# Decoder step on one NeuronCore: two of the four weight sums of a tile pair by accumulating transfers in SBUF, the third as a difference

## The chip, the cores and the metric

The kernel runs on 1 core of one Trainium2 chip. TensorE (PE) multiplies, VectorE (DVE), ScalarE (ACT) and GpSimd (POOL) work on elements, and SyncE (SP) issues most of the DMA transfers. The time is the device time of the program in microseconds. The median of three runs of the kernel before is 1004.09 us (1002.97 to 1006.44).

## The reference

One layer of a hybrid decoder step, all in float32, for a prompt of 512 rows and 8 sequences of 8 rows (576 rows in all), model width 1024:

```python
h = _rmsnorm(x, norm1_g) * (1.0 + sc1) + sh1
proj = h @ w_in
b_gate, c_gate, xa, q, k, v, ga, gb = jnp.split(proj, cuts, axis=-1)
...
yb = o @ w_attn_out
mixed = jax.nn.sigmoid(ga) * ya + jax.nn.sigmoid(gb) * yb
x = x + g1 * (mixed @ w_mix_out)
h2 = _rmsnorm(x, norm2_g) * (1.0 + sc2) + sh2
a, val = jnp.split(h2 @ w_up, 2, axis=-1)
ac, new_ffn = _causal_conv(a, ffn_buf, ffn_conv_w)
x = x + g2 * ((jax.nn.gelu(ac, approximate=False) * val) @ w_down)
```

The change concerns two of these products: the gate logits `ga` and `gb` (16 tiles of 128 columns of `w_in`), and the up projection `h2 @ w_up` (2816 gate columns and 2816 value columns, 22 tiles each).

## The kernel before, in words

Weights come in tiles of 1024 rows by 128 columns, as 128 partitions x 8 blocks x 128 (512 KB); activations stand as 8 slices of 128 partitions x 576. A float32 operand is split into a high part (rounded by ACT) and a low part (the rest, by DVE), and each product takes three passes: high by high, low by high, high by low.

**A pair of tiles.** The gate logits and most of the up projection are computed two column tiles at a time, by a scheme of seven products in place of eight (`pair_product`, L334). For tiles A and B, each cut into its first four blocks (a0, b0) and its last four (a1, b1), and the activations cut likewise and into two halves of 288 columns, it needs the weights a0, a1, b1 and four sums: S1 = b0 + b1, S2 = a0 + S1, S4 = a1 + S2, S3 = a0 + b0. The seven parts use, in this order, a0, S2, S1, a1, b1, S3, S4; each is 4 blocks x 3 passes = 12 matmuls of 288 columns. `pair_product` runs `steps[n]()` behind part n; these steps prepare the weights of the next pair while PE works on this one.

**Preparing a pair** (`pair_weights`, L283). `ra` and `rb` are the two raw tiles. `sums1` makes S3 in a buffer of its own and S1 in place of b0; `sums2` makes S2 in place of a0 and S4 in place of a1; all four are DVE additions of 128x512. Four splits follow, each a high part on ACT (`ah`, `bh`, `ch`, `dh`) and a low part on DVE (`al`, `bl`, `cl`, `dl`): A is (a0, a1), B is (S1, b1), C is (S2, S4), D is S3. A, B and C are 128x1024, D is 128x512. A raw tile may be overwritten by the next load when its last low part is made. The raw buffers are four (`W_BUFS`, L35), so two pairs are held, and the buffers for the tiles of a split are five (`S_BUFS`).

**Where pairs occur.** Eight pairs in the stage of the gates: `gate_raws(n)` loads the two raw tiles, `in_turn` (L329) gives the order of the steps, and a pair's results go through `sigmoid_pair` (DVE combines, ACT sigmoids). Eighteen pairs in the FFN, tiles 4 to 21 of the gate and of the value part (`FfnPair`, L1529). They run in three groups of 4, 8 and 6 pairs (loop at L1707), and behind each group stands a stretch of the down projection. `beside_pair` (L1581) gives the order in which the next pair's preparation and the last pair's elementwise work (first tap, two more taps, GELU, product with the value part, split) stand behind the parts.

**What sets the order.** PE, ACT and DVE are kept in program order in these stages (`pinned`, `InOrder` at L101), so a wait at one instruction holds all that stands behind it on that engine. For SP and POOL a planner sets the order (L1803). All raw tiles are loaded by SP (`load_w`, L145). In these stages POOL does a few 64-column and 16-column operations for each FFN pair and nothing for the gate pairs.

Of the kernel before, what the change touches and what calls it, by code (L numbers as in the profile page):

```python
# [13 lines left out]
ALU = mybir.AluOpType  # L14
AX = mybir.AxisListType

P = 128
D = 1024
NK = D // P
# [50 lines left out]
def step_kernel(ctx: ExitStack, tc: tile.TileContext, ins: dict, outs: list):  # L70
# [43 lines left out]
    pe, act, dve, pool = (InOrder(e) for e in (nc.tensor, nc.scalar, nc.vector, nc.gpsimd))  # L114
# [30 lines left out]
    def load_w(src, nk):  # L145

        raw = wp.tile([P, nk, P], F32, tag="raw", name=nm("raw"), bufs=W_BUFS)
        nc.sync.dma_start(raw, src)
        return raw
# [39 lines left out]
    def drain():  # L189
        while filler:  # L190
            if next(filler[0], True):
                filler.clear()
# [90 lines left out]
    def pair_weights(ra, rb):  # L283

        c0, c1 = slice(0, 4), slice(4, 8)
        w = {}

        def add(out, x, y):
            dve.tensor_tensor(out=out, in0=x, in1=y, op=ALU.add)

        def tiles():
            return [wp.tile([P, NK, P], F32R, tag=t, name=nm(t), bufs=S_BUFS) for t in ("whi", "wlo")]

        def high(name, src, get):
            w[name] = hi, lo = get()
            act.activation(hi, src, AF.Copy)

        def low(name, src):
            hi, lo = w[name]
            dve.tensor_tensor(out=lo, in0=src, in1=hi.bitcast(F32), op=ALU.subtract)  # L300

        def s3_slots():
            return slot("wh", F32R, [P, 4, P]), slot("wl", F32R, [P, 4, P])

        def sums1():
            w["raw"] = slot("s3", shape=[P, 4, P])
            add(w["raw"], ra[:, c0], rb[:, c0])
            add(rb[:, c0], rb[:, c0], rb[:, c1])

        def sums2():  # L310
            add(ra[:, c0], ra[:, c0], rb[:, c0])
            add(ra[:, c1], ra[:, c1], ra[:, c0])

        def named(n0, n1, name):
            hi, lo = w[name]
            w[n0] = (lambda k: hi[:, k, :]), (lambda k: lo[:, k, :])
            if n1:
                w[n1] = (lambda k: hi[:, k + 4, :]), (lambda k: lo[:, k + 4, :])

        def one(name, src, get, n0, n1):  # L320
            return (lambda: (high(name, src(), get), named(n0, n1, name))), (lambda: low(name, src()))

        ah, al = one("A", lambda: ra, tiles, "a0", "a1")
        dh, dl = one("D", lambda: w["raw"], s3_slots, "s3", None)
        bh, bl = one("B", lambda: rb, tiles, "s1", "b1")
        ch, cl = one("C", lambda: ra, tiles, "s2", "s4")
        return w, dict(sums1=sums1, sums2=sums2, ah=ah, al=al, bh=bh, bl=bl, ch=ch, cl=cl, dh=dh, dl=dl)

    def in_turn(t):  # L329

        order = {0: "sums1 ah al", 2: "dh dl sums2", 3: "bh bl", 4: "ch cl"}
        return {at: (lambda names=names: [t[n]() for n in names.split()]) for at, names in order.items()}

    def pair_product(w, x, steps, out_a0, out_a1, out_b0, out_b1):  # L334
# [44 lines left out]
    def kpm(w, m0, k0=0, nk=NK):  # L379
        return w[k0 * P : (k0 + nk) * P, m0 : m0 + P].rearrange("(k p) m -> p k m", p=P)  # L380
# [391 lines left out]
    def queries(t, ps=None):  # L772
# [53 lines left out]
        out=sel,  # L826
# [388 lines left out]
    ya, made = [], {}  # L1215
    wco, wao = ins["w_conv_out"][0], ins["w_attn_out"][0]
    gate_cols = [c + m * P for c in (4608, 5632) for m in range(0, NK, 2)]
    raws = {}

    def gate_raws(n):  # L1220
        if n < len(gate_cols):
            raws[n] = [load_w(kpm(w_in, gate_cols[n] + c), NK) for c in (0, P)]

    def conv_out(m, w):
        ps = product(w, gcv)
        t = slot("ya")
        act.copy(t, ps)
        ya.append(t)
# [6 lines left out]
    w_last = weights(kpm(wco, (NK - 1) * P), NK)  # L1235
    gate_raws(0)
    pinned += [pe, act, dve]
    w, steps = pair_weights(*raws[0])
    steps = in_turn(steps)
    for n in sorted(steps):  # L1240
        steps[n]()
    gate_raws(1)
    conv_out(NK - 1, w_last)
    drain()
    sg, o = [], []
    w_next = {}
# [5 lines left out]
    def gated(m):  # L1252

        if sg[m] is not None:
            dve.tensor_tensor(out=ya[m], in0=ya[m], in1=sg[m], op=ALU.mult)
            sg[m] = None

    for n in range(len(gate_cols)):
        if n + 1 < len(gate_cols):
            gate_raws(n + 2)  # L1260
            after, steps = pair_weights(*raws[n + 1])
            steps = in_turn(steps)
            if n >= 4:
                steps[5] = lambda m=2 * n - 8: gated(m)
                steps[7] = lambda m=2 * n - 7: gated(m)
        else:
            w_next[0] = weights(kpm(wao, 0), NK)
            raw = load_w(kpm(wao, P), NK)
            steps = {
                0: lambda: gated(6), 1: lambda: gated(7), 3: lambda: part_o(2), 4: lambda: part_o(3),  # L1270
                5: lambda: w_next.update({1: split_w(raw)}), 6: lambda: part_o(5), 7: lambda: part_o(7),
            }
        if n + 1 == len(gate_cols):
            fill(modulations(), 2 / 28)
        sg += sigmoid_pair(w, steps)
        w = after
# [17 lines left out]
    def residual(ps, xt, blk, c0=0, c1=NT):  # L1294

        p1 = min(c1, 512)
        dve.scalar_tensor_tensor(
            out=xt[:, c0:p1], in0=ps[:, : p1 - c0], scalar=modT[:, blk, 0:1], in1=xt[:, c0:p1],
            op0=ALU.mult, op1=ALU.add,
        )  # L1300
        if c1 > 512:
            t = sp.tile([P, 64], F32, tag="rt", name=nm("rt"))
            dve.tensor_tensor(
                out=b8(t), in0=b8(ps[:, p1 - c0 :]), in1=bc(modT[:, blk, 1:9]), op=ALU.mult
            )
            dve.tensor_tensor(out=sv(xt), in0=sv(xt), in1=t, op=ALU.add)
# [271 lines left out]
                out[at] = lambda fs=fs: [f() for f in fs]  # L1578
        return out

    def beside_pair(p, t):  # L1581

        none = lambda: None
        f = lambda n: t[n] if t else none
        g = lambda n: getattr(p, n) if p else none
        return {
            0: [f("ah"), g("first_tap"), f("sums1"), f("al"), g("taps")],
            1: [f("dh"), f("bh"), g("gelu")],
            2: [f("dl"), f("sums2"), f("bl"), g("times")],
            4: [f("ch"), g("high"), f("cl"), g("low")],  # L1590
        }

    def down_load(m, m0, m1):
# [46 lines left out]
    def value(t, ps):  # L1640
        t.times(ps)
        t.high()
# [35 lines left out]
    low()  # L1678
    ops[2].low()
    steps = pair.prepare()  # L1680
    nxt = FfnPair(5)
    ops[3].sums()
    ops[3].high()
    steps["ah"]()
    a3 = product(w_a3, h2)
    value(tiles[2], v2)
    tiles[2].low()
    ops[3].low()
    steps["sums1"]()
    steps["al"]()  # L1690
    steps["dh"]()
    steps["bh"]()
    steps["dl"]()
    v3 = product(w_v3, h2)
    start(tiles[3], a3)
    steps["sums2"]()
    tiles[3].taps()
    tiles[3].gelu()
    steps["ch"]()
    steps["bl"]()  # L1700
    steps["cl"]()
    value(tiles[3], v3)
    tiles[3].low()
# [3 lines left out]
    for m0, m1 in FCH:  # L1707
# [3 lines left out]
        for m in range(max(m0, 4), m1):  # L1711
            pair = pairs.pop(m)
            beside = [{0: n3}] if m == 4 else []
            if m + 1 < m1:
                if m + 2 < m1:
                    pairs[m + 2] = FfnPair(m + 2)
                beside.append(beside_pair(before, pairs[m + 1].prepare()))
            else:
                wd = {}
                raw = [down_load(j, m0, m1) for j in range(2)]  # L1720
                beside.append(beside_pair(before, None))
                beside.append({2: [lambda: wd.update({0: split_w(raw[0])})],
                               4: [lambda: wd.update({1: split_w(raw[1])})]})
            pair.run(merged(*beside))
            before = pair
# [6 lines left out]
        if m1 < NF:  # L1732
            pairs = {m1: FfnPair(m1)}
            steps = None
            ps = [mmps() for _ in range(2)]
            n = m1 - m0
            for k0, k1 in ((0, n - 2), (n - 2, n)):
                for j in range(2):
                    for k in range(k0, k1):
                        kstep(halves(ps[j]), wd[j], fa, k)  # L1740
            wd[2] = split_w(down_load(2, m0, m1))
            for j in range(2):
                residual(pf(ps[j]), x1[j], 40 + j)
            for m in range(2, NK):
                if m + 1 < NK:
                    wd[m + 1] = split_w(down_load(m + 1, m0, m1))
                acc_m = product(wd[m], fa)
                if m == 4:
                    steps = in_turn(pairs[m1].prepare())
                    steps[0]()  # L1750
                elif m > 4:
                    steps[m - 3]()
                if m == NK - 1:
                    pairs[m1 + 1] = FfnPair(m1 + 1)
                residual(acc_m, x1[m], 40 + m)
            continue
        pinned.clear()
# [77 lines left out]
```

## Time and profile before

| What | us |
|---|---|
| Median of three runs | 1004.09 |
| The profiled execution, its own time | 1004.44 |
| Its span, first to last instruction | 1002.6 |
| PE busy in the span | 982.7 |
| DVE busy | 670.3 |
| ACT busy | 442.3 |
| POOL busy | 85.7 |
| Gate pairs: 386.7 to 475.7 | 89.0 |
| FFN pairs 4 to 7: 645.1 to 690.3 | 45.2 |
| FFN pairs 8 to 15: 741.0 to 831.1 | 90.1 |
| FFN pairs 16 to 21: 881.9 to 945.7 | 63.8 |

The stretches at the bottom are read from the starts of the matmuls in the timeline. A view of groups has the line, the engine, the operation, the output and the inputs by the program's names, the shape and the count; "idle before" is time in which the engine had nothing to do ahead of the instruction, with what ended it. Nearly all DVE, ACT and PE work is shown at L109, the line of the helper that keeps engines in order, so groups are told apart by tiles: `raw` is a raw weight tile or a sum made in its place, `s` the buffer of S3, `whi` and `wlo` the split parts of A, B and C, `wh` and `wl` those of S3, `uv`, `p`, `pad`, `sg` and `cy` the combinations of the seven products. SPq and POOLq are DMA issues.

### The profile page before, as it was taken

Reading aid. Unit: us, or ns where it says so; the run is one execution under the profiler, and the core shown is the slowest. Engines: PE = TensorE matmul, PEld = TensorE weight load, DVE = VectorE, ACT = ScalarE, POOL = GpSimd, SP = SyncE. Lnnn points to the kernel's source line nnn. Section 1 sums busy time; section 2 is a strip of 40 time slices with the busy share of each in tenths; the row PEclk is TensorE's granted clock in tenths of the full one; section 3 lists DMA queues with packets and bytes.
Section 4 is the critical chain, followed back from the end, with each engine's and each line's share of the span. In section 5 each row is a group of like instructions: output and inputs, shape, how many; then the busy total and the mean of one; then the engine's idle time right before and its main releaser. Section 6 shows DMA issues by size and latency. Waiting matters only on the chain.

```text
span 1002.6 us, 18686 instructions
## 1 busy us (share of the span) xinstructions
PE 982.7 (98%) x7502; PEld 941.9 (94%) x7502; DVE 670.3 (67%) x1244; ACT 442.3 (44%) x831; POOL 85.7 (9%) x241
## 2 busy tenths in 40 slices
PE   7999999999999999999999999999999999999996
PEld 5898999999989889999889999999999999999996
DVE  5736766665653367888463568896559995579944
ACT  5454545444534335454242348554225543235433
POOL 2210000000010000000000022011001110001121
PEclk9999999999999999999999999999999999999999
DMA  9993323333413932225973302223233322323302
GB/s 285 321 251 99 96 75 86 86 115 106 152 58 83 304 106 84 85 86 154 359 213 87 109 1 74 75 84 107 78 97 96 88 85 85 105 64 100 117 24 95
DMA packets 176424, 119.70 MB, mean 119 GB/s; under 512 B 8943, under 2 KB 162766, under 8 KB 176050
## 3 DMA queue, kind: packets, MB, share of 16 engines
q1 hardware_dynamic: 174482, 111.06, 37.4%
q0 software_dynamic: 1856, 7.44, 2.1%
q8 instruction: 59, 0.97, 0.4%
q14 instruction: 27, 0.22, 0.1%
HBM read 109.69 MB, written 7.35 MB: 117 GB/s over the span
## 4 chain that ended last, share of the span: by engine, by line
PE 86%; DVE 7%; ACT 2%; DMA 2%; issue 1%; SPq 0%; POOL 0%; DVEq 0%; ACTq 0%
PE mm L109 62%; PE aux L109 21%; DVE wlo L109 2%; PE aux L1099 2%; PE aux L1014 1%; DMA raw<-in_w_in 1%; DVE raw L109 1%; DMA ad<-in_w_ada 1%; DMA q<-low 1%; DVE cy L109 0%; ACT whi L109 0%; DVE y L109 0%; DVE uv L109 0%; SPq L385 0%; DMA con<-in_consts 0%
## 5 line engine op out<-in xcount | busy, mean ns | idle before, releaser
L109 ACT ACTIVATE whi<-raw 128x1024 fp32r<-128x1024 f32 (+2 forms) x164 | 168.0, 1034 | 200.7 <-PE mm L109 109.4
L109 DVE TENSOR_TENSOR wlo<-raw,whi 128x1024 fp32r<-128x1024 f32 (+2 forms) x164 | 195.2, 1195 | 46.9 <-ACT whi L109 45.2
L109 PE MATMUL mm<-hh,whi 128*128 128x256 f32 (+2 forms) x560 | 127.7, 305 | 0.6 <-ACT hh L109 0.6
L109 PE MATMUL mm<-hh,wlo 128*128 128x256 f32 (+2 forms) x560 | 122.3, 295 | 0.0
L109 PE MATMUL mm<-hl,whi 128*128 128x256 f32 (+2 forms) x560 | 121.1, 295 | 0.0
L109 PEld LDWEIGHTS mm<-hh,whi 128*128 128x128 f32 x560 | 91.7, 189 | 8.3 <-issue 6.6
L109 PEld LDWEIGHTS mm<-hh,wlo 128*128 128x128 f32 x560 | 94.3, 188 | 0.0
L109 PEld LDWEIGHTS mm<-hl,whi 128*128 128x128 f32 x560 | 93.7, 188 | 0.4 <-DVE hl L109 0.4
L109 DVE SCALAR_TENSOR_TENSOR x<-mm,modT,x 128x512 f32<-128x512 f32 (+1 forms) x33 | 22.6, 685 | 79.0 <-PE mm L109 79.0
L109 PE MATMUL mm<-fl,whi 128*128 128x256 f32 (+1 forms) x304 | 65.3, 296 | 0.0
L109 PE MATMUL mm<-fh,wlo 128*128 128x256 f32 (+1 forms) x304 | 65.1, 295 | 0.0
L109 PE MATMUL mm<-fh,whi 128*128 128x256 f32 (+1 forms) x304 | 65.1, 296 | 0.0
L109 PE MATMUL mm<-th,whi 128*128 128x288 f32 x208 | 61.8, 297 | 0.6 <-DVE uv L109 0.5
L109 PE MATMUL mm<-th,wlo 128*128 128x288 f32 x208 | 61.5, 296 | 0.5 <-DVE wlo L109 0.5
L109 PE MATMUL mm<-tl,whi 128*128 128x288 f32 x208 | 61.4, 295 | 0.0
L109 PEld LDWEIGHTS mm<-fl,whi 128*128 128x128 f32 x304 | 51.0, 189 | 0.0
L109 PEld LDWEIGHTS mm<-fh,wlo 128*128 128x128 f32 x304 | 50.9, 188 | 0.1
L109 PEld LDWEIGHTS mm<-fh,whi 128*128 128x128 f32 x304 | 50.6, 188 | 0.1
L109 PE MATMUL aux<-2h,whi 128*128 128x288 f32 (+2 forms) x160 | 47.4, 296 | 0.8 <-ACT p L109 0.8
L109 PE MATMUL aux<-2h,wlo 128*128 128x288 f32 (+2 forms) x160 | 47.5, 297 | 0.0
L109 PE MATMUL aux<-2l,whi 128*128 128x288 f32 (+2 forms) x160 | 47.2, 295 | 0.0
L865 ACT ACTIVATE s<-s,nmx 128x256 f32<-128x256 f32 (+1 forms) x72 | 34.0, 475 | 27.4 <-DVE nmx L862 27.4
(302 smaller groups left out, 2547.5 us busy)
## 6 DMA issues: line engine op xcount, KB each, us to landing
raw<-in_w_in SPq DMA_DIRECT2D x52, 512.0 KB, 4.8
raw<-in_w_up SPq DMA_DIRECT2D x44, 512.0 KB, 3.9
ada<-in_w_ada SPq DMA_DIRECT2D x64, 256.0 KB, 6.0
ad<-in_w_ada SPq DMA_DIRECT2D x32, 256.0 KB, 6.5
raw<-in_w_down SPq DMA_DIRECT2D x16, 512.0 KB, 3.6
raw<-in_w_conv_out SPq DMA_DIRECT2D x8, 512.0 KB, 3.6
raw<-in_w_attn_out SPq DMA_DIRECT2D x8, 512.0 KB, 3.6
raw<-in_w_mix_out SPq DMA_DIRECT2D x8, 512.0 KB, 5.8
```

The lines of the kernel that those rows point to most:

```text
L109: done = getattr(self.engine, name)(*args, **kwargs)
L865: nc.scalar.activation(s[x // 2][:, x % 2, :w], s[x // 2][:, x % 2, :w], AF.Exp, bias=nmx[:, x : x + 1], accum_out=den[:, x : x + 1],)
L1014: done = nc.tensor.matmul(O[HALF[par], :256], vt(i - nkt + 1 + kt)[:, hd * 64 : hd * 64 + 64], pts[kt][:, par * 256 : par * 256 + 256], st ...
L1099: done = nc.tensor.matmul(ps[32 * j : 32 * j + 32, :], cT[:, k, :], cols[k][j], start=(k == 1), stop=(k == NK - 2),)
```

## The change

S1 and S4 are no longer DVE additions. Each becomes a transfer from SBUF to SBUF that adds into its destination, issued by POOL: S1 adds b1 into b0, and S4 adds S2 into a1. S2 stays a DVE addition, and now needs S1. S3 is now a DVE subtraction, S2 - b1, which equals a0 + b0. The order of the steps follows: for the gates A and S2 come first, then S3 and B, then D, then C (before: S3, S1 and A, then D, S2 and S4, then B, then C). S1 of a pair is issued one pair earlier, behind part 6 of the gates and behind part 5 of the FFN pairs. So the next pair's loads and `pair_weights` are called earlier in the program. In the gates the multiplications `gated` move from part 5 to part 3 for the first of two.

```diff
-        def add(out, x, y):
-            dve.tensor_tensor(out=out, in0=x, in1=y, op=ALU.add)
+        def add_to(out, x):
+            pool.dma_start(out, x, accum_op=ALU.add)
...
-        def sums1():
+        def s1():
+            add_to(rb[:, c0], rb[:, c1])
+
+        def s2():
+            dve.tensor_tensor(out=ra[:, c0], in0=ra[:, c0], in1=rb[:, c0], op=ALU.add)
+            add_to(ra[:, c1], ra[:, c0])
+
+        def s3():
             w["raw"] = slot("s3", shape=[P, 4, P])
-            add(w["raw"], ra[:, c0], rb[:, c0])
-            add(rb[:, c0], rb[:, c0], rb[:, c1])
-
-        def sums2():
-            add(ra[:, c0], ra[:, c0], rb[:, c0])
-            add(ra[:, c1], ra[:, c1], ra[:, c0])
+            dve.tensor_tensor(out=w["raw"], in0=ra[:, c0], in1=rb[:, c1], op=ALU.subtract)
...
-        order = {0: "sums1 ah al", 2: "dh dl sums2", 3: "bh bl", 4: "ch cl"}
+        order = {0: "ah al s2", 2: "s3 bh bl", 4: "dh dl", 5: "ch cl"}
...
+            first_sum = prep[n + 2][1]["s1"] if n + 2 in prep else lambda: None
             if n >= 4:
-                steps[5] = lambda m=2 * n - 8: gated(m)
+                steps[3] = lambda m=2 * n - 8: gated(m)
                 steps[7] = lambda m=2 * n - 7: gated(m)
+            steps[6] = first_sum
...
-            0: [f("ah"), g("first_tap"), f("sums1"), f("al"), g("taps")],
-            1: [f("dh"), f("bh"), g("gelu")],
-            2: [f("dl"), f("sums2"), f("bl"), g("times")],
-            4: [f("ch"), g("high"), f("cl"), g("low")],
+            0: [f("ah"), g("first_tap"), f("al"), f("s2"), g("taps")],
+            1: [f("bh"), g("gelu")],
+            2: [f("s3"), f("bl"), g("times")],
+            4: [f("dh"), g("high"), f("dl"), g("low")],
+            5: [f("ch"), f("cl"), after["s1"] if after else none],
...
                 elif m > 4:
-                    steps[m - 3]()
+                    steps[2 * m - 10]()
                 if m == NK - 1:
+                    steps[5]()
                     pairs[m1 + 1] = FfnPair(m1 + 1)
+                    pairs[m1 + 1].prepare()["s1"]()
```

The rest of the diff places the same steps around the first pair of each stage.

More of the change, by code (lines that the diff above doesn't have):

```diff
@@ L326, in pair_weights @@
         ch, cl = one("C", lambda: ra, tiles, "s2", "s4")
-        return w, dict(sums1=sums1, sums2=sums2, ah=ah, al=al, bh=bh, bl=bl, ch=ch, cl=cl, dh=dh, dl=dl)
+        return w, dict(s1=s1, s2=s2, s3=s3, ah=ah, al=al, bh=bh, bl=bl, ch=ch, cl=cl, dh=dh, dl=dl)
     def in_turn(t):
-        order = {0: "sums1 ah al", 2: "dh dl sums2", 3: "bh bl", 4: "ch cl"}
+        order = {0: "ah al s2", 2: "s3 bh bl", 4: "dh dl", 5: "ch cl"}
         return {at: (lambda names=names: [t[n]() for n in names.split()]) for at, names in order.items()}
@@ L1217, in step_kernel @@
     gate_cols = [c + m * P for c in (4608, 5632) for m in range(0, NK, 2)]
-    raws = {}
+    prep = {}
     def gate_raws(n):
         if n < len(gate_cols):
-            raws[n] = [load_w(kpm(w_in, gate_cols[n] + c), NK) for c in (0, P)]
+            prep[n] = pair_weights(*[load_w(kpm(w_in, gate_cols[n] + c), NK) for c in (0, P)])
     def conv_out(m, w):
@@ L1237, in step_kernel @@
     pinned += [pe, act, dve]
-    w, steps = pair_weights(*raws[0])
+    w, steps = prep[0]
+    steps["s1"]()
     steps = in_turn(steps)
@@ L1243, in step_kernel @@
     conv_out(NK - 1, w_last)
+    prep[1][1]["s1"]()
     drain()
@@ L1260, in step_kernel @@
             gate_raws(n + 2)
-            after, steps = pair_weights(*raws[n + 1])
+            after, steps = prep[n + 1]
             steps = in_turn(steps)
+            first_sum = prep[n + 2][1]["s1"] if n + 2 in prep else lambda: None
             if n >= 4:
-                steps[5] = lambda m=2 * n - 8: gated(m)
+                steps[3] = lambda m=2 * n - 8: gated(m)
                 steps[7] = lambda m=2 * n - 7: gated(m)
+            steps[6] = first_sum
         else:
@@ L1579, in merged, with beside_pair @@
         return out
-    def beside_pair(p, t):
+    def beside_pair(p, t, after=None):
         none = lambda: None
@@ L1680, in step_kernel @@
     steps = pair.prepare()
+    steps["s1"]()
     nxt = FfnPair(5)
@@ L1686, in step_kernel @@
     value(tiles[2], v2)
+    steps["al"]()
+    steps["s2"]()
     tiles[2].low()
     ops[3].low()
-    steps["sums1"]()
-    steps["al"]()
-    steps["dh"]()
     steps["bh"]()
-    steps["dl"]()
+    steps["bl"]()
+    steps["s3"]()
     v3 = product(w_v3, h2)
     start(tiles[3], a3)
-    steps["sums2"]()
+    steps["dh"]()
+    steps["ch"]()
+    steps["dl"]()
     tiles[3].taps()
     tiles[3].gelu()
-    steps["ch"]()
-    steps["bl"]()
+    nxt.prepare()["s1"]()
     steps["cl"]()
@@ L1714, in step_kernel @@
             if m + 1 < m1:
+                after = None
                 if m + 2 < m1:
                     pairs[m + 2] = FfnPair(m + 2)
-                beside.append(beside_pair(before, pairs[m + 1].prepare()))
+                    after = pairs[m + 2].prepare()
+                beside.append(beside_pair(before, pairs[m + 1].steps, after))
             else:
@@ L1749, in step_kernel @@
                     steps = in_turn(pairs[m1].prepare())
-                    steps[0]()
+                    pairs[m1].steps["s1"]()
                 elif m > 4:
-                    steps[m - 3]()
+                    steps[2 * m - 10]()
                 if m == NK - 1:
+                    steps[5]()
                     pairs[m1 + 1] = FfnPair(m1 + 1)
+                    pairs[m1 + 1].prepare()["s1"]()
                 residual(acc_m, x1[m], 40 + m)
```

## The prediction

> **What bounds the kernel now.** I read the page first (its span and busy lines), then the busy time of each engine by stretch, then the timeline of PE inside the FFN stretches.
>
> ```profile
> span 1002.6 us, 18686 instructions
> PE 982.7 (98%) x7502; PEld 941.9 (94%) x7502; DVE 670.3 (67%) x1244; ACT 442.3 (44%) x831; POOL 85.7 (9%) x241
> ```
> ```profile
> 386.70:475.70 89.00, 89.00 (x674) 89.00 (x673) 74.33 (x109) 45.95 (x74) 0.00 (x0) 1.00 0.38 114
> 641.00:690.30 49.30, 47.82 (x357) 47.15 (x357) 45.83 (x72) 25.27 (x39) 6.64 (x22) 1.00 0.34 97
> 741.00:831.10 90.10, 89.60 (x674) 89.16 (x673) 85.69 (x135) 46.28 (x67) 12.37 (x43) 1.00 0.30 89
> 881.90:945.70 63.80, 63.80 (x484) 63.76 (x482) 60.27 (x96) 33.26 (x49) 8.17 (x28) 1.00 0.26 75
> ```
>
> The columns of the second fence are the stretch and its length, then busy time and count of PE, PEld, DVE, ACT and POOL, the granted clock, the DMA share and GB/s. The clock is 1.00 everywhere, so it plays no part. PE is the bound: the eight gate pairs take 89.00, 11.13 us for a pair of 84 matmuls. In the gates PE never idles, so DVE work taken out there can gain nothing. In the FFN stretches DVE is nearly full, and PE has small holes. These are the holes (start, length, operation; in brackets the idle time and what ended it):
>
> ```profile
> 645.20 0.29 PE L109 MATMUL mm<-tl,whi 128*128 128x288 f32 x1
> 646.03 0.40 PE L109 MATMUL mm<-th,wlo 128*128 128x288 f32 x1 [0.54 <-DVE wlo L109]
> ...
> 650.04 0.40 PE L109 MATMUL aux<-2h,whi 128*128 128x288 f32 x1 [0.82 <-ACT p L109]
> ...
> 680.22 0.29 PE L109 MATMUL aux<-2h,wlo 128*128 128x288 f32 x1
> 680.63 0.37 PE L109 MATMUL mm<-th,whi 128*128 128x288 f32 x1
> ...
> 809.37 0.29 PE L109 MATMUL aux<-2h,wlo 128*128 128x288 f32 x1
> 809.90 0.37 PE L109 MATMUL mm<-th,whi 128*128 128x288 f32 x1 [0.23 <-DVE uv L109]
> ...
> 820.96 0.29 PE L109 MATMUL aux<-2h,wlo 128*128 128x288 f32 x1
> 821.52 0.37 PE L109 MATMUL mm<-th,whi 128*128 128x288 f32 x1 [0.26 <-DVE uv L109]
> ```
>
> Matmuls follow each other every 0.13 us (89.00 / 674), so the starts lost are 0.83 - 0.13 = 0.70, about 0.9 (0.82 idle and a slower first matmul), 0.28, 0.40 and 0.43, in all 2.7; with a slower first matmul behind the first ones as well some 3.2. **That is the ceiling of any gain**: 0.32% of the time.
>
> **Part 1: the additions leave DVE.** One FFN pair on DVE, from product to product (start, length, operation):
>
> ```profile
> 787.22 0.45 DVE L109 TENSOR_TENSOR uv<-mm,uv 128x288 f32<-128x288 f32 x1
> 787.59 0.68 DVE L109 TENSOR_TENSOR s<-raw,raw 128x512 f32<-128x512 f32 x1
> 788.31 0.69 DVE L109 TENSOR_TENSOR raw<-raw 128x512 f32<-128x512 f32 x1
> 788.92 1.22 DVE L109 TENSOR_TENSOR wlo<-raw,whi 128x1024 fp32r<-128x1024 f32 x1
> ...
> 792.63 0.80 DVE L109 TENSOR_TENSOR raw<-raw,raw 128x512 f32<-128x512 f32 x1
> 793.47 0.69 DVE L109 TENSOR_TENSOR raw<-raw 128x512 f32<-128x512 f32 x1
> 794.08 1.22 DVE L109 TENSOR_TENSOR wlo<-raw,whi 128x1024 fp32r<-128x1024 f32 x1
> ...
> 798.84 0.45 DVE L109 TENSOR_TENSOR uv<-mm,uv 128x288 f32<-128x288 f32 x1
> ```
>
> DVE's period is 798.84 - 787.22 = 11.62 against PE's 11.13, so DVE falls back by 0.5 us a pair until PE waits for `uv`. The four sums take 788.92 - 787.59 = 1.33 and 794.08 - 792.63 = 1.45. Two stay (2 x 0.69), so the period becomes 11.62 - 2.78 + 1.38 = 10.22, below PE's. The stalls at 680, 809 and 821 end in `uv` and are a result of that drift; they go: 0.28 + 0.40 + 0.43 = 1.1, with the refill some 1.35. Of the two at the entry to the first FFN group, which wait for `wlo` and ACT's `p`, I take 1.0 of about 1.85, since the entry has the same steps with two sums fewer. Gain: 2.4.
>
> **Part 2: 52 transfers come onto POOL's queue.** Two for each of 26 pairs. POOL's own cost for one is its issue, of which there is a row:
>
> ```profile
> 478.02 0.55 POOL L1325 DMA_DIRECT2D x<-xT_dram  x1 [147.19 <-DVE ol L109]
> ```
>
> 52 x 0.55 = 28.6 us on an engine that is busy 85.7 of 1002.6; it waits anyway, so nothing for throughput. But order on POOL counts: for each pair it first issues S1 of the pair after next, which waits for that raw tile's load, and then S4 of the next pair. A late load therefore holds S4, and behind S4 stand the 64-column operations (`cy`) of the FFN.
>
> **Part 3: how long one lasts, L.** No accumulating transfer and none from SBUF to SBUF is in the trace. Its time from issue to landing is bounded by these rows (output and input, queue, count, KB each, median us to landing):
>
> ```profile
> raw<-in_w_up SPq DMA_DIRECT2D x44, 512.0 KB, 3.9
> xT_dram<-xT POOLq DMA_DIRECT2D x4, 576.0 KB, 6.1
> x<-xT_dram POOLq DMA_DIRECT2D x2, 1152.0 KB, 8.5
> out<-yo SPq DMA_DIRECT2D x8, 256.0 KB, 2.3
> out<-so POOLq DMA_DIRECT2D x7, 32.0 KB, 1.8
> ```
>
> The transfer has 256 KB, 128 x 512 float32. From below 2.3, the same bytes out of SBUF on SP's queue with no reading of the destination. From above 6.1, a POOL transfer of 576 KB, a little more than the 512 KB that are read (source and destination). In between, the POOL rows of 32 KB (1.8) and 1152 KB (8.5) give 6.7 / 1120 = 0.0060 us per KB; with 512 KB read, 1.8 + 512 x 0.0060 = 4.9. I take 4.9, because it is the one that uses POOL's queue at this size and counts both operands; with 256 KB alone the same line gives 3.3. DMA itself is not full (0.26 to 0.38).
>
> The Trainium skill ("DMA: Bandwidth & Descriptors", Anatomy of one DMA — SWDGE (gpsimd) path) fits a GpSimd transfer as 2.0 us plus its bytes at 436 GB/s; as an estimate 2.6 us here, between the rows' ends, and by it the time would be that of rival 1 below. The fit is for transfers that do not add, and no run before shows one that does.
>
> **Part 4: the new wait in the gates.** Before, C was made from S2 and S4 of DVE, one behind the other. Now `s4` is on the way for L, and ACT's `ch` waits for it, DVE's `cl` for `ch`. DVE and ACT are in program order. Behind `cl` stand the combinations of the pair that PE has just finished (v, b0, b1, then a1), behind these the sigmoid on ACT and the next `ah`, `al`, `s2`, and then the next `s4`: a loop over one pair. Its links (the last two rows are groups: count, busy and mean ns, then idle before):
>
> ```profile
> 440.99 0.45 DVE L109 TENSOR_TENSOR uv<-mm,p 128x288 f32<-128x288 f32 x1
> ...
> 441.84 0.45 DVE L109 TENSOR_TENSOR sg<-uv,p 128x288 f32<-128x288 f32 x1
> ...
> 442.56 0.46 DVE L109 TENSOR_TENSOR sg<-mm,uv 128x288 f32<-128x288 f32 x1 [0.27 <-PE mm L109]
> ```
> ```profile
> 442.38 1.12 ACT L109 ACTIVATE sg<-sg 128x576 f32<-128x576 f32 x2 [3.23 <-issue]
> 443.40 1.05 ACT L109 ACTIVATE whi<-raw 128x1024 fp32r<-128x1024 f32 x1
> ```
> ```profile
> L109 DVE TENSOR_TENSOR raw<-raw 128x512 f32<-128x512 f32 x14 | 9.7, 692 | 0.5
> L109 DVE TENSOR_TENSOR wlo<-raw,whi 128x1024 fp32r<-128x1024 f32 x24 | 29.4, 1224 | 8.8 <-ACT whi L109 8.4
> ```
>
> ch 1.05, cl 1.22, v to b1 1.30 (440.99 to 442.29), a1 0.46, then from 443.02 (a1's end) to 444.45 (`ah`'s end) 1.43, al 1.22, s2 0.69: 7.37, and about 0.3 of hand-offs between engines: 7.7 + L. Against 11.13 it is hidden up to **L = 3.4**. At 4.9 the loop takes 12.6, and each turn loses 1.47.
>
> How much of that is free the first time: PE starts a run of pairs at 386.70 + 5 x 11.125 = 442.33, and `ah` ends 443.40 + 1.05 - 442.33 = 2.1 into the run, so `s4` goes out at 2.1 + 1.22 + 0.69 = 4.05, and `cl` ends at 4.05 + 4.9 + 1.05 + 1.22 = 11.2. PE needs the bank that v clears at the second part of the next pair, 11.13 + 12 x 0.13 = 12.7, v takes 0.45: limit 12.2. Slack 0.95 us. Pairs 1 to 7 are made inside the loop, so six turns follow the first: 6 x 1.47 - 0.95 = **7.9 us lost**. With the slack the loss over all turns is 7 L - 26.4, so it begins at L = 3.8, not at 3.4.
>
> **Part 5: the loads' loop in the FFN.** The elementwise work of an FFN pair stands ahead of `ch`, so the loop above does not close there (DVE's 10.22 leaves room). Another does: a raw tile is free when `cl` has read it, then 3.9 for the load of the tile that takes its place, POOL's issue of S1 that waits for it 0.55, then `s4` behind it on the same queue L, ch 1.05, cl 1.22: 6.7 + L, hidden up to 4.4. At 4.9 it is 11.6, 0.5 too long; four turns in the group of eight lose 2.0, two in the group of six 1.0. The first `cl` ends at about 5.2 + 4.9 = 10.1, 2.1 ahead of the same limit: **nothing lost**, the load's lead is used up. Before, that lead was large:
>
> ```profile
> 785.50 0.37 SPq L148 DMA_DIRECT2D raw<-in_w_up  x1
> ```
>
> 785.50 + 4.9 (this one's own landing, later than the median) is 790.4, and the next pair needs it near 797.
>
> **The sum.** Part 1 -2.4, part 2 0, part 4 +7.9, part 5 0: +5.5. On the profiled execution, 1004.44 by its own time (span 1002.6), 1009.9; it stands 0.35 above the median, so **1009.6** against 1004.09.
>
> **Rivals.** 0.3% is 3.0 us, about what a measurement of this kernel tells from no change; faster means below 1001.1, slower above 1007.1.
>
> *Rival 1, the other side: the transfers are hidden.* If L is at most 3.8, both loops fit, the gates' with their slack, and only part 1 is left: 1004.1 - 2.4 = 1001.7, or 1000.9 when all 3.2 of the holes close. For it: 256 KB from SP land in 2.3, and one operand only on POOL's line gives 3.3. Against it: POOL's 576 KB took 6.1, and the add reads twice the bytes. It decides at L = 3.8. Chance 0.30, of which 0.12 falls below 1001.1 and 0.18 within 0.3%.
>
> *Rival 2: the FFN's loads chain too.* From L = 5.5 on. At 5.5 the gates lose 7 x 5.5 - 26.4 = 12.1, the FFN group of eight 4 x 1.07 - 1.5 = 2.8 and the group of six 2 x 1.07 - 1.5 = 0.6: 15.5 - 2.4 = +13.1, 1017. At the upper end 6.1: 16.3, 4 x 1.67 - 0.9 = 5.8 and 2.4, less 2.4: +22.1, 1026. For it: S1 and S4 go out close together on one queue while two loads of 512 KB run, and 6.1 was measured when four POOL transfers ran close together. Chance 0.22.
>
> *Rival 3: POOL's issue itself is slowed by DVE*, which is busy 84 to 95% in these stretches; the 0.55 row fell in a stretch where it was not. If an issue waits for one or two splits (1.22 each), L becomes 6.1 to 7.3; each 1 us costs 7 in the gates and 4 + 2 in the FFN: 1026 to 1042. Nothing in the trace speaks for it. Chance 0.06.
>
> That the DVE additions would not go away is excluded: the program of the changed kernel has 52 of them fewer. That they go and gain nothing, as PE's holes stay at the entries, is inside the first rival (1004).
>
> **How the numbers follow.** Forecast 0.42 (L from 3.8 to 5.4, where the same sums give 1002 to 1015; 0.06 of it within 0.3%), rival 1 0.30, rival 2 0.22, rival 3 0.06. Faster 0.12; same 0.18 + 0.06 = 0.24; slower 0.64. The range runs from rival 1 with nearly all holes closed, 1001.0, to rival 2 at its upper end, 1027. The likeliest case alone spans 1002 to 1015.
>
> **What would show it.** In the DMA issues, `raw` from `raw` on POOL's queue, 26 twice, with L. DVE busy near 670.3 - 26 x 1.4 = 634. In the gates PE's time for a pair above 11.13 from the third or fourth on, holes at the second part that end in DVE's `uv`, ACT's `whi` waiting for the DMA. In the FFN, no holes at 680, 809, 821. Wrong if L is below 3.8 (gates stay 89.0), if `s1` waits for its load ahead of `s4` so long that POOL's order and not L sets the loop, or if the clock in these stretches falls below 1.00.

## The result, and the profile after

The changed kernel takes 1014.84 us (median of 4 runs, 1013.34 to 1017.39) against 1003.53 of the kernel before. The ratio on record, 1.0104 with a 95% interval of 1.008 to 1.0127, lies a little below the quotient of these two medians, 1.0113. A second set of six runs (below, `e9_changed_again`) gave 1012.04 against 1004.13, ratio 1.0082 (1.0061 to 1.0104). So it is slower by about 8 to 11 us; 1009.6 was predicted. The profiled execution took 1013.83, span 1011.7: 9.1 above the span before.

The page of the changed kernel: span, busy times, and the group and the DMA row of the new transfers (count, busy and mean ns, idle before; then KB each and median us to landing):

```profile
span 1011.7 us, 18812 instructions
...
PE 985.4 (97%) x7502; PEld 943.9 (93%) x7502; DVE 637.6 (63%) x1192; ACT 442.0 (44%) x831; POOL 140.0 (14%) x293
...
L109 POOL DMA_DIRECT2D raw<-raw x52 | 45.2, 903 | 277.5 <-DVE raw L109 78.4
...
raw<-raw POOLq DMA_DIRECT2D x52, 256.0 KB, 3.4
```

Busy times by stretch (columns as in the prediction):

```profile
386.70:475.70 89.00, 85.74 (x638) 84.77 (x638) 56.42 (x84) 42.51 (x67) 11.02 (x13) 1.00 0.56 127
641.00:690.30 49.30, 46.51 (x349) 46.08 (x348) 39.93 (x62) 25.48 (x40) 14.33 (x30) 1.00 0.51 116
741.00:831.10 90.10, 88.48 (x665) 87.87 (x664) 73.11 (x113) 42.72 (x61) 27.90 (x55) 1.00 0.57 133
881.90:945.70 63.80, 63.80 (x483) 63.66 (x482) 50.55 (x79) 30.45 (x44) 19.21 (x38) 1.00 0.56 130
```

DVE is 33 us less busy, as the change means. The holes that it was to close in the FFN are closed, but PE has new ones, and for the first time some in the gates (timeline of PE):

```profile
435.96 0.37 PE L109 MATMUL mm<-th,whi 128*128 128x288 f32 x1 [0.77 <-DVE uv L109]
448.10 0.37 PE L109 MATMUL mm<-th,whi 128*128 128x288 f32 x1 [0.69 <-DVE uv L109]
460.37 0.37 PE L109 MATMUL mm<-th,whi 128*128 128x288 f32 x1 [0.88 <-DVE uv L109]
...
664.30 0.37 PE L109 MATMUL mm<-th,whi 128*128 128x288 f32 x1 [0.90 <-DVE uv L109]
...
677.54 0.37 PE L109 MATMUL mm<-th,whi 128*128 128x288 f32 x1 [1.89 <-DVE uv L109]
...
807.59 0.37 PE L109 MATMUL mm<-th,whi 128*128 128x288 f32 x1 [0.74 <-DVE uv L109]
```

All end in DVE's `uv`: the second part of a pair waits for the combination v of the last one, as the prediction had it. Setting each matmul's start against the same matmul before tells where the 9.1 us are. Some 1.8 stand ahead of the change, 1.5 of them at 86 to 90 us, where the granted clock was 0.57 in this execution (not in the second one). The gates and their exit lose 5.2 (4.8 up to 475.7). The entry to the FFN gains 1.9. The first FFN group then loses 2.9 net, the group of eight 1.2 net of the holes of before that are gone, the group of six nothing.

**The chain in the gates.** One turn on POOL, ACT and DVE of the changed kernel:

```profile
452.19 0.84 POOL L109 DMA_DIRECT2D raw<-raw  x1 [10.15 <-DVE wlo L109]
453.38 0.85 POOL L109 DMA_DIRECT2D raw<-raw  x1 [0.35 <-DVE uv L109]
```
```profile
457.54 1.06 ACT L109 ACTIVATE whi<-raw 128x1024 fp32r<-128x1024 f32 x1 [3.05 <-DMA raw<-raw]
...
469.80 1.06 ACT L109 ACTIVATE whi<-raw 128x1024 fp32r<-128x1024 f32 x1 [3.10 <-DMA raw<-raw]
```
```profile
452.16 0.69 DVE L109 TENSOR_TENSOR raw<-raw,raw 128x512 f32<-128x512 f32 x1
...
458.63 1.23 DVE L109 TENSOR_TENSOR wlo<-raw,whi 128x1024 fp32r<-128x1024 f32 x1 [2.41 <-ACT whi L109]
459.77 0.45 DVE L109 TENSOR_TENSOR uv<-mm,p 128x288 f32<-128x288 f32 x1
```

S2 ends at 452.85, `s4` goes out at 453.38 (0.53 later) and `ch`, waiting for it, starts at 457.54 (4.16 later); then `cl`, then v at 459.77, and PE goes on at 460.37. One turn is 469.80 - 457.54 = 12.26 us against PE's 11.13; the prediction had 12.6. The first POOL row is S1 of the pair after next, ahead of S4 on the queue.

**The chain in the FFN.** SP's load, POOL's two issues (x2 is S1 and S4), then ACT and SP's next load:

```profile
795.03 0.37 SPq L148 DMA_DIRECT2D raw<-in_w_up  x1
...
807.11 0.37 SPq L148 DMA_DIRECT2D raw<-in_w_up  x1
```
```profile
799.46 1.78 POOL L109 DMA_DIRECT2D raw<-raw  x2 [3.05 <-DMA raw<-in_w_up]
```
```profile
804.76 1.06 ACT L109 ACTIVATE whi<-raw 128x1024 fp32r<-128x1024 f32 x1 [1.09 <-DMA raw<-raw]
```

POOL waited for the load, not for S2, which had ended at 798.39. S1 went out at 799.46, S4 at 800.04, and `ch` started 4.72 later. From load to load it is 12.08 us: the loop of the prediction's part 5, at 11.6 there.

The first FFN group, where the largest hole is (677.54), shows the same pair of issues (x2) and the wait behind them:

```profile
668.38 1.78 POOL L109 DMA_DIRECT2D raw<-raw  x2 [3.19 <-DMA raw<-in_w_up]
```
```profile
674.71 2.00 ACT L109 ACTIVATE whi<-raw 128x1024 fp32r<-128x1024 f32 x2 [2.18 <-DMA raw<-raw]
```

S1 went out at 668.38, S4 at 669.10, and `ch` could start at 674.71 only.

### The profile page after: what moved, and what is told of

The parts are those of the page before. It is cut to its first block, busy times and chain, and to the rows that moved or that the text cites. A ratio compares the mean times of both kernels' runs of the same rounds, so it can differ in the third digit from the quotient of the medians.

```text
span 1011.7 us, 18812 instructions
## 1 busy us (share of the span) xinstructions
PE 985.4 (97%) x7502; PEld 943.9 (93%) x7502; DVE 637.6 (63%) x1192; ACT 442.0 (44%) x831; POOL 140.0 (14%) x293
## 4 chain that ended last, share of the span: by engine, by line
PE 69%; DMA 10%; DVE 7%; ACT 4%; issue 4%; POOL 1%; DVEq 0%; POOLq 0%; ACTq 0%
PE mm L109 54%; PE aux L109 13%; DMA raw<-raw 5%; DVE wlo L109 3%; ACT whi L109 2%; PE aux L1102 2%; DMA raw<-in_w_up 2%; DMA raw<-in_w_in 1%; PE aux L1017 1%; DMA snk<-in_attn_sinks 1%; DVE uv L109 1%; DMA q<-low 1%; ACT sg L109 0%; DVE ol L109 0%; DVE y L109 0%
## 5 line engine op out<-in xcount | busy, mean ns | idle before, releaser
L109 POOL DMA_DIRECT2D raw<-raw x52 | 45.2, 903 | 277.5 <-DVE raw L109 78.4
L109 PEld LDWEIGHTS mm<-th,whi 128*128 128x128 f32 x208 | 39.1, 188 | 9.8 <-ACT whi L109 5.1
```

The lines of the kernel that those rows point to most:

```text
L109: done = getattr(self.engine, name)(*args, **kwargs)
```

## The experiments

The theory from these two chains was that the loss is what waits for S4's transfer, and S1 ahead of it on POOL's queue makes that wait longer (the flight theory). Against it stood the new order of the steps (order theory) and the bytes moved inside SBUF (traffic theory).

**S1 by transfer, S4 on DVE.**

```diff
-            add_to(ra[:, c1], ra[:, c0])
+            dve.tensor_tensor(out=ra[:, c1], in0=ra[:, c1], in1=ra[:, c0], op=ALU.add)
```

> S4 goes back to DVE, S1 stays a transfer; the order of the steps is that of the changed kernel. Flight theory (the loss comes from what waits for S4's transfer: its flight of about 4.0 us, and in the FFN S1 ahead of it on POOL's queue): nothing waits for S1, which is issued one pair early, and DVE has one addition less (11.62 - 0.69 = 10.9 us a pair, below PE's 11.13). Both the gates' 5 us and the FFN's 3.5 us of loss go, the gain of the FFN's holes stays: 2 to 3 us below the kernel before, 1001 to 1002. Order theory (the new order of the steps, S3 as a difference and C last, makes the loss): as slow as the changed kernel, 1011 to 1015. Traffic theory (the bytes moved inside SBUF slow loads and engines): half of the bytes, half of the loss, 1007 to 1010.

Measured 1003.22 against 1004.24, ratio 0.9983 (0.9971 to 0.9995); span 1001.4. The gates have no hole (PE 89.00 of 89.00), the loss is gone, with half of the transfers. But only 1.2 us is gained in the stages of the change by the starts of the matmuls, where 2 to 3 were expected. DVE's period, from `uv` to `uv`, is still 11.61, as before, though it has one addition less:

```profile
809.75 0.45 DVE L109 TENSOR_TENSOR uv<-mm,uv 128x288 f32<-128x288 f32 x1
...
821.36 0.45 DVE L109 TENSOR_TENSOR uv<-mm,uv 128x288 f32<-128x288 f32 x1
```

**S4 by transfer, S1 on DVE** (where DVE waits for ACT anyway).

```diff
-            add_to(rb[:, c0], rb[:, c1])
+            dve.tensor_tensor(out=rb[:, c0], in0=rb[:, c0], in1=rb[:, c1], op=ALU.add)
...
+        al = lambda: (s1(), al_())
```

> S1 goes back to DVE, ahead of the low part of A, where DVE waits for ACT; S4 stays a transfer. Flight theory: with no S1 ahead of it on the queue, S4 lands 3.3 us after its issue in place of 4.0 to 4.6, the gates' loop falls from 12.2 to 11.5 us, which its slack covers but for 0 to 1 us, and in the FFN no transfer waits for a load: 1001 to 1003. Order theory: 1011 to 1015. Traffic theory: half of the loss, 1007 to 1010. If S4's flight is 4.0 whether or not S1 is ahead of it, the gates keep their 4.5 us and the time is 1005 to 1007.

Measured 1005.92, ratio 1.0019 (1.0005 to 1.0033): better than the changed kernel by 6 to 9 us, but above what was expected. A turn in the gates is now the distance of two POOL rows:

```profile
437.30 0.84 POOL L109 DMA_DIRECT2D raw<-raw  x1 [10.82 <-DVE uv L109]
448.98 0.85 POOL L109 DMA_DIRECT2D raw<-raw  x1 [10.84 <-DVE uv L109]
```

It is 11.68, and the flight is 3.5 (448.98 to 452.53). That is still longer than PE's 11.13, so the last three pairs lose 0.3 to 0.6 us each; the rest is lost at the exit of the gates and in the first FFN group, where a hole of 1.2 us stands at the second pair.

**All sums on DVE, in the new order.**

```diff
         def s1():
-            add_to(rb[:, c0], rb[:, c1])
+            pass
         def s2():
+            dve.tensor_tensor(out=rb[:, c0], in0=rb[:, c0], in1=rb[:, c1], op=ALU.add)
             dve.tensor_tensor(out=ra[:, c0], in0=ra[:, c0], in1=rb[:, c0], op=ALU.add)
-            add_to(ra[:, c1], ra[:, c0])
+            dve.tensor_tensor(out=ra[:, c1], in0=ra[:, c1], in1=ra[:, c0], op=ALU.add)
```

> All sums on DVE, in the order of the changed kernel (S3 as a difference, C last, S1 and S4 on either side of S2 on DVE). Flight theory and traffic theory: no transfer, no loss, and DVE as full as before (11.62 us a pair), so the holes of the kernel before are there again: 1002 to 1006. Order theory: 1011 to 1015.

Measured 1011.53, ratio 1.0074 (1.0061 to 1.0087). This speaks for the order theory, but elsewhere than the changed kernel loses:

```profile
386.70:475.70 89.00, 89.00 (x674) 89.00 (x673) 72.54 (x106) 45.92 (x73) 0.00 (x0) 1.00 0.35 104
...
741.00:831.10 90.10, 86.86 (x648) 85.82 (x647) 82.19 (x128) 43.84 (x63) 14.82 (x40) 1.00 0.30 88
```
```profile
790.70 0.45 DVE L109 TENSOR_TENSOR uv<-mm,uv 128x288 f32<-128x288 f32 x1
...
800.61 1.23 DVE L109 TENSOR_TENSOR wlo<-raw,whi 128x1024 fp32r<-128x1024 f32 x1 [0.19 <-ACT whi L109]
...
802.91 0.45 DVE L109 TENSOR_TENSOR uv<-mm,uv 128x288 f32<-128x288 f32 x1
```

The gates have no hole at all, so their loss in the changed kernel isn't the order's. In the FFN DVE's period is 802.91 - 790.70 = 12.21 with the same four sums that took 11.62 before: the new order costs DVE 0.6 us a pair, partly in waits for ACT's high parts (0.19 here, 0.21 at `fl`). It fits only when DVE has less to do, which also explains the first experiment: 12.21 - 0.6 or so for one addition is 11.6. The expectation had put this at nothing.

**S4 ahead of S1 on POOL's queue.** All 52 transfers stay; POOL keeps the program's order, in which S4 of the next pair comes first. This holds for POOL's small operations in the FFN too.

```diff
-    pinned += [pe, act, dve]
+    pinned += [pe, act, dve, pool]
...
-            pinned.extend([dve, act])
+            pinned.extend([dve, act, pool])
```

> The changed kernel with POOL's transfers kept in the order of the program: S4 of the next pair goes out before S1 of the pair after it, which no longer stands ahead of it on the queue. All 52 transfers stay. Flight theory: S4's flight falls from 4.0 to 4.6 to about 3.3, the gates' loop to 11.5, and in the FFN S4 no longer waits for a load; 1001 to 1003.5. Order theory and traffic theory: no change against the changed kernel, 1011 to 1015. If only the FFN recovers, as S4's flight does not depend on S1, 1007 to 1010.

Measured 1003.96, ratio 1.0008 (0.9992 to 1.0023); span 1000.2, 2.4 below the kernel before, of which 1.9 stand ahead of the change. This settles most of it: the same transfers and the same order on PE, ACT and DVE, and the loss is gone but for the end of the gates.

```profile
386.70:475.70 89.00, 88.06 (x661) 87.66 (x660) 63.09 (x94) 44.34 (x71) 11.15 (x13) 1.00 0.62 137
...
741.00:831.10 90.10, 90.10 (x683) 90.10 (x683) 79.71 (x122) 47.12 (x67) 22.97 (x58) 1.00 0.59 132
```
```profile
447.43 1.72 POOL L109 DMA_DIRECT2D raw<-raw  x2 [9.87 <-DVE uv L109]
...
459.35 0.84 POOL L109 DMA_DIRECT2D raw<-raw  x1 [10.20 <-ACT sg L109]
```

The group of eight is full (90.10 of 90.10), more than before (89.60). In the gates S4 now flies 3.4 us (447.43 to 450.83), a turn is 11.6 to 11.9, and PE loses 1.3 us at the last two pairs, when the slack is used up. The traffic theory falls: the transfers are all there. Their traffic isn't free, though: the S1 that follows S4 lands 5.3 us after its issue, and a load of 512 KB that starts 1.1 us behind it in the gates takes 5.75 us, where most such loads took 4.1 to 4.3 in the changed kernel; neither is waited for.

**S4 first, and in the gates on DVE.**

```diff
+            if gates:
+                dve.tensor_tensor(out=ra[:, c1], in0=ra[:, c1], in1=ra[:, c0], op=ALU.add)
+            else:
                 add_to(ra[:, c1], ra[:, c0])
```

> The changed kernel with S4 ahead of S1 on POOL's queue as in e4_s4_first, and in the gates S4 on DVE as in e1_s1_only; in the FFN both sums stay transfers. If the gates' loss is the flight of S4 alone, the gates show no hole (1.4 us less than e4_s4_first), and the FFN has e4_s4_first's gain of 2 to 3 us: 1001 to 1002, 2 to 3 us below the kernel before. If the S1 transfers hurt the gates by their traffic, 1 us of holes stays in the gates and the time is 1002.5 to 1004.

Measured 1002.75 against 1003.85, ratio 0.9985 (0.9971 to 1.0); span 999.7. The gates have no hole:

```profile
386.70:475.70 89.00, 89.00 (x671) 89.00 (x670) 70.12 (x101) 45.83 (x74) 5.05 (x6) 1.00 0.44 119
641.00:690.30 49.30, 48.73 (x368) 48.48 (x367) 42.33 (x67) 25.22 (x39) 10.81 (x27) 1.00 0.59 140
741.00:831.10 90.10, 90.10 (x682) 90.10 (x682) 79.65 (x121) 47.13 (x67) 22.73 (x58) 1.00 0.59 132
```

The span is 2.9 us shorter, 0.45 of it ahead of the change and some 0.2 behind the last matmul. By the starts of the matmuls the stages of the change gain 2.2, near the 2.4 that the prediction had put for part 1: 2.7 in the FFN, less 0.45 in the gates, which are slower by 0.06 us a pair without a hole. The runs with S1 alone, with half of the columns and with plain copies show this 0.45 too; all sums on DVE in the same order show 0.05. So it comes with the transfers; why is open. The runs' medians differ by 1.1, less than expected, and the interval just reaches 1, so it beats the kernel before by 0.3% at most. It ties with the first experiment.

**What the flight is made of.** Three runs of the changed kernel's order, with other transfers. Half of the columns (half of S1 and of S4 is not added):

```diff
-            add_to(rb[:, c0], rb[:, c1])
+            add_to(rb[:, 0:2], rb[:, 4:6])
...
-            add_to(ra[:, c1], ra[:, c0])
+            add_to(ra[:, 4:6], ra[:, 0:2])
```

> The changed kernel with each transfer cut to its first two blocks, 128 partitions x 256 in place of 128 x 512: half of S1 and half of S4 are not added. Two S1 and S4 one behind the other land 1.95 us apart in the changed kernel, and a lone one lands 3.3 us after its issue. If these 1.95 us are moved bytes: about 1.0 apart, alone 2.4, an S4 behind an S1 at 3.0 to 3.4, so the gates' loop is 8.2 + 3.2 = 11.4 and the loss nearly goes: 1001 to 1004. If they are a cost of each row or of each transfer: still 1.95 apart, and 1010 to 1014.

Half of the partitions (the sums of the other 64 are left out):

```diff
-            add_to(rb[:, c0], rb[:, c1])
+            add_to(rb[:64, c0], rb[:64, c1])
...
-            add_to(ra[:, c1], ra[:, c0])
+            add_to(ra[:64, c1], ra[:64, c0])
```

> The changed kernel with each transfer cut to 64 of its 128 partitions, with all four blocks: half of the bytes and half of the rows; the sums of the other 64 partitions are left out. If a transfer's time goes by bytes, as e5_half: about 1.0 us apart, alone 2.4. If it goes by rows: the same here, but not in e5_half. If by neither, 1.95 apart and 3.3 alone in both.

Plain copies (no sums):

```diff
-            add_to(rb[:, c0], rb[:, c1])
+            pool.dma_start(rb[:, c0], rb[:, c1])
...
-            add_to(ra[:, c1], ra[:, c0])
+            pool.dma_start(ra[:, c1], ra[:, c0])
```

> The changed kernel with plain copies of the same size in place of the accumulating transfers (S1 and S4 are then b1 and S2, not sums). If reading the destination is half of the time, as the prediction's 512 KB had it: alone 2.4, two of them 1.0 us apart, little loss (1001 to 1004). If the add costs nothing beside the issue on POOL's queue: alone 3.3, 1.95 apart, and 1011 to 1015.

The DMA rows, in this order:

```profile
raw<-raw POOLq DMA_DIRECT2D x52, 128.0 KB, 2.7
```
```profile
raw<-raw POOLq DMA_DIRECT2D x52, 128.0 KB, 3.2
```
```profile
raw<-raw POOLq DMA_DIRECT2D x52, 256.0 KB, 2.3
```

| Transfer | alone, us | second lands behind first, issues 0.6 apart | time |
|---|---|---|---|
| adding, 128 x 512 | 3.3 | 1.7 to 2.5, mostly 1.9 | 1014.84, 1012.04 |
| adding, 128 x 256 | 2.7 | 0.9 | 1002.19, ratio 0.9982 (0.997 to 0.9993) |
| adding, 64 x 512 | 3.2 | 1.3 to 2.2 | 1006.98 (one run) |
| plain, 128 x 512 | 2.3 | 0.8 | 1001.26 (one run) |

The add costs 1.0 us of flight, and the queue then delivers one transfer every 1.9 us in place of 0.8. It isn't the bytes as such: half of the columns halve the distance of two, half of the partitions leave it at 1.3 to 1.5 in most FFN pairs and at 1.9 and 2.2 twice in the gates, and hardly shorten a lone one. With half of the columns or with plain copies the loss is gone although S1 still stands ahead of S4: gates and FFN stretches are full in both traces. With half of the partitions S4 stays late in the gates, which lose 4.6 us, while the groups of eight and six have no hole (S4 mostly flies 3.8 to 4.1 there). None of the three cases of the expectation for half of the partitions came about; whether the length of a row sets the time or the 64 partitions are served by fewer DMA engines was not tried apart.

**The changed kernel once more.**

> The changed kernel once more, without an edit, as its first profile has a stretch at 86 to 90 us, far ahead of the change, where the granted clock was 0.57 and PE lost 1.75 us. If that belongs to one execution and not to the change: the stretch is not there or not at that place, the span is 1009 to 1010.5, and the ratio to the kernel before is 1.006 to 1.009. If it belongs to the change, the clock falls there again, the span is near 1011.7, the ratio 1.010 or more. In either case the gates lose 4.5 us in four or five holes that end in DVE's uv, and the FFN loses 2 us net of what it gains.

Measured 1012.04, ratio 1.0082 (1.0061 to 1.0104); span 1010.3. The stretch at 86 to 90 us runs at clock 1.00, so those 1.5 us belong to one execution. But there is a larger hole in the gates, and a low clock behind that:

```profile
423.90 0.58 PE L109 MATMUL mm<-th,whi 128*128 128x288 f32 x1 [2.72 <-DVE uv L109]
```
```profile
414.33 1.75 POOL L109 DMA_DIRECT2D raw<-raw  x2 [11.51 <-DVE s L109]
```
```profile
424.00:428.00 4.00, 4.00 (x20) 4.00 (x21) 2.30 (x5) 3.21 (x5) 0.31 (x1) 0.62 0.45 133
```

One load, issued at 408.18, took 5.6 us here in place of 4.0. S1, which waits for it, went out at 414.33, and S4 behind it only at 415.20, though S2 had ended at 413.37; it flew 5.8 us. So POOL's order passes a late load on to PE in the gates too. The hole was 3.0 us, and PE then ran some 3.0 us at about half of its clock (matmuls 0.24 us apart in place of 0.13). By the starts of the matmuls the gates lose 7.7 us here up to 475.7, some 1.4 of them by that clock, against 4.8 in the first profile; without the late load's hole (3.0) and the clock it is 3.3. From its entry on the FFN loses 0.6 net, against 2.2 in the first: 1.9 gained at the entry, 2.2 lost in the first group, 0.4 in the group of eight. Both were expected to be as in the first profile and are not. In the gates the late load and the clock make the difference; for the FFN no cause is shown.

## Why the prediction came out right, and where its steps failed

The sign and the place were right: S4's flight in a loop through `ch`, `cl`, v and the next `s2`, with holes at the second part that end in DVE's `uv`, and a second loop through the loads. The size was right partly by luck, by errors that cancel: the forecast was +7.9 in the gates and -2.4 in the FFN; by the starts of the matmuls the first profile has +5.2 (with the exit) and +2.2, the second +8.2 and +0.6.

**Part 1 (gain 2.4).** DVE's busy time fell to 637.6 (634 forecast). The gain is there: 2.2 us in the trace of S4 first with the gates on DVE. The step to a period of 10.22 left out that the new order costs DVE 0.6 us a pair (12.21 against 11.62 with all sums on DVE); 10.8 is still below 11.13, so the sum did not suffer.

**Part 2 (0.55 an issue).** Plain copies took 0.54 at the median, adding ones 0.87: 45.2 us in all for 28.6. No engine was short for it. But that a late load holds S4 was told and then priced at nothing. That is the step that failed. In the FFN turn shown above S4 went out 1.65 us behind S2's end in place of 0.53, as it stood behind the load's hand-off (0.57) and S1's issue (0.58), and behind S1 it flew 4.6 in place of 3.3.

**Part 3 (L = 4.9).** A lone transfer takes 3.3, an S4 behind an S1 3.7 to 4.1 in the gates and 4.3 to 5.5 in the FFN, where the two go out 0.6 to 0.9 us apart. By rival 1's own bound, 3.8, a lone one would have been nearly hidden, and the median of the DMA row (3.4, S1 and S4 mixed) looks as if rival 1 had held. The bounds from the rows held (2.3 is what the plain copy takes), but the value taken was too high for one transfer, and the queue's 1.9 us between two was missing. The trace before had a queue to read: the four POOL transfers behind the row of 6.1 went out 0.5 to 0.7 us apart, and they took 3.8, 5.8, 6.5 and 7.5 us in this order. The prediction's own line at 256 KB, 3.3, would have met a lone one. By the fit of the Trainium skill ("DMA: Bandwidth & Descriptors", Anatomy of one DMA — SWDGE (gpsimd) path) the estimate for 256 KB is 2.6 us; the plain copy's 2.3 is near it, the adding one's 3.3 is not covered by it.

**Part 4 (7.9 lost in the gates).** Measured 4.8, with the exit 5.2, in the first profile. The turn was 12.26 and not 12.6: L was 0.9 us lower, while the 0.3 of hand-offs were 0.8 (0.53 alone from S2's end to POOL's issue). The prediction's form, six turns less the slack, gives 6 x 1.1 - 1.4 = 5.2 with these values, with 8.2 + 4.0 for the turn and 1.4 for the slack.

**Part 5 (nothing lost in the FFN).** Measured some 5.5 us of new holes, 2.2 net of the gains; in the second profile 0.6 net. The loop is 12.08 and not 11.6: beside L there are 7.4 us and not 6.7, because of 0.57 from the load's landing to S1's issue and hand-offs. And the first group, for which the prediction counted no turn, lost most (1.1 and 2.1 us at 664 and 677): its first S4 goes out at 657.40, late in the run, since DVE still splits the operands there, and the second S4 then flew 5.5 us behind S1.

**The rivals.** Rival 1 failed by the queue and the hand-offs, not by L: with S4 alone on the queue, at 3.5, the gates still lost 1.8. Each of the prediction's own signs of being wrong came in part: a lone L below 3.8, though the gates did not stay at 89.0; in the FFN S1's wait for its load, which set when S4 went out; and in the second profile a clock of 0.62 in 4 us of the gates. Rival 2's mechanism, the loads' chain, is what happened in the FFN, at a lower L than the 5.5 it was given. Rival 3 has nothing for it: plain copies were issued in 0.54 us in the same stretches beside a DVE that was busier (79.1 us in the group of eight against 73.1 in the changed kernel).

## What to carry to other kernels

A transfer that takes work from a busy engine must be priced as a place in a queue: what stands ahead of it there, what that waits for, and how fast the queue delivers. Here putting S4 ahead of S1, which nobody waited for, was worth all of the 8 to 11 us. An engine that is not the bound gives little back when it is relieved, here 2.2 of 1004 us, while each hand-off on the new path (0.5 us) is paid in every turn of the loop; write the loop down and compare it with the bound's period before moving anything into it.

## What was not expected of the hardware

An adding transfer inside SBUF of 128 x 512 float32 takes 3.3 us and its issue 0.87, a plain one 2.3 and 0.54; two adding ones land 1.9 us apart, two plain ones 0.8. Cutting the columns to half saves 0.6 us of the lone one, cutting the partitions to half 0.1.

After a hole the clock sometimes falls. In the changed kernel's first profile PE had waited 1.94 us ahead of 85.38, and this followed:

```profile
86.00:88.00 2.00, 2.00 (x11) 2.00 (x10) 1.11 (x5) 0.95 (x5) 0.00 (x0) 0.56 0.05 14
88.00:90.00 2.00, 2.00 (x12) 2.00 (x11) 0.00 (x0) 0.80 (x5) 0.00 (x0) 0.58 0.00 0
```

In the second it was the 3.0 us hole at 421. But the length of the hole alone does not decide: 1.75 us ahead of 85.10 in the kernel before and 1.89 ahead of 677.54 in the changed kernel were not followed by it, nor was this longer one in the run with all sums on DVE, where the clock stayed at 1.00:

```profile
86.16 0.36 PE L109 MATMUL aux<-kh,q 128*128 128x256 f32 x1 [2.60 <-DMA q<-low]
```

The Trainium skill ("TensorE: Matmul & The Clock Gate", Part 1: The HAM clock gate) has the clock fall to half after an idle window of about 3.4 us; here it fell once behind 1.94 us and not behind 2.60. What decides between one hole and the next is left open.
